# Seven pairs of input strips as seven block products each, and a triangular inversion in two blocks with its corner on TensorE

## The chip, the cores and the metric

The kernel runs on one core of a Trainium2 chip. The metric is the device time of one execution in microseconds (us), the median of several runs. Before the change it is 2264.03 us (three runs, 2262.74 to 2264.18). A second table of numbers comes from one profiled execution, whose times are counted from its first instruction.

## The reference

One decoder layer on 1024 tokens of width 1024, in float32: a SwiGLU half-step (ffn1), a mixer of three branches, and a second SwiGLU half-step (ffn2), each between two RMS norms. Cut to the mixer, which the change touches:

```python
u = rms_norm(h, mix_pre_g[l])
p_rwkv, p_swa, q_mem, gate_logits = _split(u @ w_in[l], IN_SIZES)
y_a = rwkv7_mix(p_rwkv, ...)            # recurrence over 1024 steps, 8 heads of 64
y_b = sliding_window_gqa_sinks(...)     # from p_swa, window 128
y_c = memory_cross_attention(...)       # from q_mem, 256 memory tokens
g_a, g_b, g_c = _split(jax.nn.sigmoid(gate_logits + gate_b[l]), (D, D, D))
merged = g_a * (y_a @ w_branch[l, 0]) + g_b * (y_b @ w_branch[l, 1]) + g_c * (y_c @ w_branch[l, 2])
h = h + rms_norm(merged @ w_out[l], mix_post_g[l])
```

## The kernel before, in words

**Products.** Activations lie feature-major: 8 blocks of 128 features (k) by 1024 tokens, in two halves of 512 (h = 0, 1). A float32 operand is split into a high part (a rounded copy, made by ScalarE, ACT: `w_hi`, line 288, or `split`, line 472) and a low part (the difference, made by VectorE, DVE: line 290 or 473). `mm3` (lines 364 to 366) makes a product of three matmuls: high by high, high by low, low by high. A *strip* is 128 output columns of a weight; `project` runs one strip over 8 k-blocks and both halves, 48 matmuls of 128x512. Weights come through five `w_raw` buffers of 256 KB (`raw`), and up to eight split operands are kept ahead of TensorE (PE) (`prefetch`); the order of the weights is `plan`'s list. DMAs of weights and results are nearly all issued by one in-order queue, SyncE's (SP).

**The feed-forward layers** already use a form of block product: two strips, two halves of K and two halves of the tokens are a 2x2 by 2x2 block product, made of seven products of 12 matmuls instead of eight, with sums of the weights (lines 315 to 321 for kind "pair") and sums of the input (`factors_part`, `factors_end`) made beside them, and sums of the results on the way out (`ffn_in_pair`).

**The mixer.** The `w_in` product has 48 strips: 14 for the recurrence (0 to 13), 10 for the two attentions (14 to 23, `att_block`), 24 for the gates (`gate_block`, a tanh on the way out). Half of strips 18, 19, 14 and 15, and four strips of the recurrence, are made earlier, while the first norm of the mixer runs. In order of the program then come:

- `rwkv_prep`: the other strips of the recurrence, their scans and norms, the triangular 64x64 matrices per chunk and head (16 chunks x 8 heads = 128 of them, products `ab`, line 1094, stored to `ab_d`), and the second halves of strips 18 and 19; `pk_d` and `bonus_d` are stored for later;
- `rwkv_invert`: all 128 matrices at once, one on each partition, loaded as rows of 64x64; 62 steps of two DVE operations (lines 1129 and 1130), each step adding an outer product of the j rows above by the 63 - j columns behind; a memset of the diagonal; one store to `inv_d`;
- strips 14 to 17 and 20 to 23, then gates 0 to 7;
- `rwkv_chain`: 16 chunks in sequence, small float32 matmuls on PE and short operations on the other engines, each chunk with its `f` and `dinv` loads; gates 8 and 9 are woven in;
- `rwkv_finish` and `attention` (8 memory blocks, 8 window blocks), between whose steps `fill(n, ...)` lets n matmuls of the remaining gates (10 to 23) and of two branches' projections pass. How many per block is written out by hand (`LUMPS` and the list in `mixer`); what is left follows the last block. `sums_beside` makes sums for ffn2's weights there.

**Order.** A scheduler orders each engine's instructions by priority (program order, moved ahead inside `high_priority(offset=...)`: 300 is `lead`, 1000 is `urgent`) as their inputs become ready; `keep_in_program_order` and `issue_after` fix single orders. Then each engine runs its list strictly. Tiles come from pools laid out from the left and the right end of each partition; a tile of a new pool waits for the last use of the tiles whose space it takes. PSUM has four banks for px, py, pgate, pq and the like, and four for the rest (pz, gram, z, y, ab).

**Norms.** `post_norm` ends in `acc` tiles, which are stored to `h1` (line 879) for the next residual; `pre_norm` (line 498) scales them into a tile `un` and splits it into u's high and low parts.

## Time and profile before

| | |
|---|---|
| three runs, median | 2264.03 us |
| profiled execution, its own span | 2260.2 us |
| TensorE busy | 2236.6 us, 99% |
| VectorE busy | 1652.0 us, 73% |
| ScalarE busy | 1000.2 us, 44% |
| DMA moved | 417.66 MB, 185 GB/s |
| granted TensorE clock, mean | 0.998 |

The profiled execution gives no time beside its span; the median of the runs is 3.8 us longer than that span. Stages by the profile: ffn1 up to about 650 us, then `rwkv_prep` to 885, inversion 908 to 1029 on VectorE beside strips and gates on PE, `rwkv_chain` 1048 to 1155, attention 1200 to 1448, ffn2's products from 1670.

How to read it: a row of a timeline has the start, the duration, the engine and line, operation and tiles, and in brackets the idle time before it and what ended it. A row of groups has the count, the busy time and the mean duration of one in ns. A row of waits has the total in us, the times, and the longest one. PE is the matmul side of TensorE and PEld its weight loads.

### The profile page before, as it was taken

How to read it: one execution, taken by the hardware profiler on the slowest of the kernel's cores; microseconds unless marked ns; L12 is line 12 of the kernel's file. 1: busy time of each engine (PE TensorE's matmuls, PEld its weight loads, DVE VectorE, ACT ScalarE, POOL GpSimd, SP SyncE). 2: the span in 40 equal slices, each digit the busy share in tenths (PEclk: the TensorE clock that was granted, in tenths of full speed). 3: DMA queues.
4: the chain of work that ended last, by engine and by line, in shares of the span. 5: the costliest groups of instructions: out<-in, count | busy, mean ns of one | idle time of the engine just before them, and what ended most of it. 6: DMA issues, size and time to landing. Idle time of an engine off the chain costs nothing.

```text
span 2260.2 us, 33447 instructions
## 1 busy us (share of the span) xinstructions
PE 2236.6 (99%) x11876; PEld 1840.4 (81%) x11876; DVE 1652.0 (73%) x2719; ACT 1000.2 (44%) x1880; POOL 58.1 (3%) x114
## 2 busy tenths in 40 slices
PE   8999999999999999999999999999999999999998
PEld 6888888888888788888888887788888888888887
DVE  6987777666698886995666576684898885656576
ACT  6533333454556653223454445334663233345451
POOL 0000000000000000001320000000000000000000
PEclk9999999999999999999999999999999999999999
DMA  8465666686654467325438885654565542347663
GB/s 291 157 210 168 215 212 208 214 276 207 191 173 149 117 143 183 118 93 194 144 113 289 266 278 186 209 177 136 173 214 188 189 168 90 116 165 250 204 196 122
DMA packets 280775, 417.66 MB, mean 185 GB/s; under 512 B 82304, under 2 KB 104320, under 8 KB 280352
## 3 DMA queue, kind: packets, MB, share of 16 engines
q1 hardware_dynamic: 272832, 400.26, 55.3%
q10 hardware_dynamic: 7776, 15.28, 2.0%
q8 instruction: 93, 1.52, 0.3%
q14 instruction: 74, 0.61, 0.1%
HBM read 284.89 MB, written 129.50 MB: 183 GB/s over the span
## 4 chain that ended last, share of the span: by engine, by line
PE 93%; DVE 4%; DMA 1%; ACT 1%; issue 1%; SPq 0%; DVEq 0%; ACTq 0%
PE px L365 7%; PE px L364 7%; PE px L366 7%; PE po L365 6%; PE po L366 6%; PE po L364 6%; PE pgate L364 4%; PE pgate L366 4%; PE pgate L365 4%; PE pz L365 3%; PE pz L364 3%; PE pz L366 3%; PE pb L364 2%; PE pb L365 2%; PE pb L366 2%; PE pr L364 2%
## 5 line engine op out<-in xcount | busy, mean ns | idle before, releaser
L288 ACT CAST w_hi<-w_raw 128x512 fp32r<-128x512 f32 x594 | 367.5, 620 | 734.5 <-PE px L365 159.7
L290 DVE TENSOR_TENSOR w_lo<-w_raw,w_hi 128x512 fp32r<-128x512 f32 x594 | 407.6, 687 | 196.0 <-ACT w_hi L288 175.2
L366 PE MATMUL po<-u,w_lo 128*128 128x512 f32 (+1 forms) x476 | 180.9, 380 | 0.0
L364 PE MATMUL po<-u,w_hi 128*128 128x512 f32 (+1 forms) x476 | 180.9, 380 | 0.0
L365 PE MATMUL po<-u,w_hi 128*128 128x512 f32 (+1 forms) x476 | 180.9, 380 | 0.0
L364 PE MATMUL pgate<-u,w_hi 128*128 128x512 f32 x384 | 153.2, 399 | 0.0
L366 PE MATMUL pgate<-u,w_lo 128*128 128x512 f32 x384 | 151.4, 394 | 0.0
L365 PE MATMUL pgate<-u,w_hi 128*128 128x512 f32 x384 | 149.8, 390 | 0.0
L365 PE MATMUL px<-f,w_hi 128*128 128x512 f32 x352 | 137.2, 390 | 1.0 <-DVE f L473 1.0
L364 PE MATMUL px<-u,w_hi 128*128 128x512 f32 x352 | 137.0, 389 | 0.8 <-DVE km L1442 0.8
L364 PE MATMUL px<-f,w_hi 128*128 128x512 f32 x352 | 137.1, 389 | 0.1
L366 PE MATMUL px<-u,w_lo 128*128 128x512 f32 x352 | 137.0, 389 | 0.0
L366 PE MATMUL px<-f,w_lo 128*128 128x512 f32 x352 | 137.0, 389 | 0.0
L365 PE MATMUL pz<-u,w_hi 128*128 128x512 f32 x352 | 137.0, 389 | 0.0
L365 PE MATMUL px<-u,w_hi 128*128 128x512 f32 x352 | 136.9, 389 | 0.0
L364 PE MATMUL pz<-u,w_hi 128*128 128x512 f32 x352 | 136.9, 389 | 0.0
L366 PE MATMUL pz<-u,w_lo 128*128 128x512 f32 x352 | 136.9, 389 | 0.0
L473 DVE TENSOR_TENSOR u<-hid,u 128x512 fp32r<-128x512 f32 x114 | 78.3, 690 | 46.5 <-ACT u L472 43.5
L364 PEld LDWEIGHTS po<-u,w_hi 128*128 128x128 f32 x476 | 89.5, 188 | 17.1
L365 PEld LDWEIGHTS po<-u,w_hi 128*128 128x128 f32 x476 | 89.5, 188 | 17.1
L366 PEld LDWEIGHTS po<-u,w_lo 128*128 128x128 f32 x476 | 89.5, 188 | 16.8
L472 ACT CAST u<-hid 128x512 fp32r<-128x512 f32 x114 | 70.7, 620 | 64.3 <-DMA hid<-form_d 55.7
(401 smaller groups left out, 5097.4 us busy)
## 6 DMA issues: line engine op xcount, KB each, us to landing
w_raw<-in_ffn_in SPq DMA_DIRECT2D x220, 256.0 KB
hid<-form_d SPq DMA_DIRECT2D x154, 256.0 KB
w_raw<-in_win SPq DMA_DIRECT2D x112, 256.0 KB
form_d<-g SPq DMA_DIRECT2D x88, 256.0 KB
w_raw<-ffn_sum_d SPq DMA_DIRECT2D x88, 256.0 KB
form_d<-h SPq DMA_DIRECT2D x66, 256.0 KB
w_raw<-in_ffn_out SPq DMA_DIRECT2D x66, 256.0 KB
gate_d<-gate SPq DMA_DIRECT2D x24, 512.0 KB
```

Of the source, the lines that this page charges most:

```text
L288: self.nc.scalar.copy(hi, x)
L290: self.split_last = self.nc.vector.tensor_tensor(lo, x, hi.bitcast(F32), ALU.subtract)
L364: mm(out, wh, xh, start=first, stop=False, **kw)
L365: mm(out, wh, xl, start=False, stop=False, **kw)
L366: self.last_mm = mm(out, wl, xh, start=False, stop=last, **kw)
L472: self.nc.scalar.copy(hi, x)
L473: self.nc.vector.tensor_tensor(lo, x, hi.bitcast(F32), ALU.subtract)
```

## The change

`pre_norm` scales the `acc` tile in place instead of into `un`, and stores it to `xn_d`. In the mixer, `mix_x` loads that input again in quarters (features low and high, tokens h = 0 and 1), four tiles for each of four k, through a pool `mix_parts` of five tiles; `mix_forms` makes four sums of them and splits each into high and low parts (32 tiles), with the lead of 300. Seven pairs of strips (16 and 17, 20 and 21, 22 and 23, and gates 2 to 9 in twos) are made by `win_pair` as seven block products; their weights get the four sums of kind "pair". Strips 14 and 15 and gates 0 and 1 stay as they are and now come first, behind `mix_forms`; then the inversion in program order, then the pairs.

The inversion runs on the two diagonal blocks of 32x32 of each matrix (30 steps of two operations, both blocks in one), stores the result, and a transposed copy of the first block to `turn_d`. Ahead of the pair with index 5, `rwkv_corner` loads the corner of the matrices and the two inverted blocks with rows on partitions (12 DMAs), multiplies them in two products of 128 small matmuls each (four groups of 32 partitions in turn), and stores the corner (4 DMAs).

Ten gates instead of eight are made ahead of the chain, the fill starts at gate 12 instead of 10, and the lumps are 42, 32, then 29 six times and 52 eight times, instead of 42, 34, 30 and 54.

```diff
-GATES_EARLY = 10
-LUMPS = (30, 54)
-GATES_FIRST = 8
+GATES_PLAIN = 2
+CORNER = 5
+GATES_FIRST = 10
+GATES_EARLY = 12
+LUMPS = (29, 52)
+WIN_PAIRS = ((16, 17), (20, 21), (22, 23)) + tuple((24 + g, 25 + g) for g in range(GATES_PLAIN, GATES_FIRST, 2))
...
-            t = pool.tile([P, TH], F32, tag="un", name="un", bufs=2)[:, : hi - lo]
-            self.nc.vector.scalar_tensor_tensor(t, xs[k], self.vec(gname, k), rs, ALU.mult, ALU.mult)
-            self.split(t, *(y[:, lo:hi] for y in u[k][h]))
+            self.nc.vector.scalar_tensor_tensor(xs[k], xs[k], self.vec(gname, k), rs, ALU.mult, ALU.mult)
+            self.split(xs[k], *(y[:, lo:hi] for y in u[k][h]))
+            self.nc.sync.dma_start(self.xn_d[:, k, h * TH + lo : h * TH + hi], xs[k])
...
+        blocks = x.rearrange("p (b r) -> p b r", b=2)[:, :, : H * C].rearrange("p b (s t) -> p b s t", t=C)[:, :, :, :H]
+        for j in range(1, H - 1):
+            n = H - 1 - j
+            tmp = pool.tile([P, H * H], F32, tag="itmp", name="itmp", bufs=1)
+            t = tmp[:, : 2 * j * n].rearrange("p (b a n) -> p b a n", b=2, n=n)
+            V.tensor_tensor(t, blocks[:, :, j : j + 1, j + 1 :].broadcast_to([P, 2, j, n]), blocks[:, :, 0:j, j : j + 1].broadcast_to([P, 2, j, n]), ALU.mult)
+            V.tensor_tensor(blocks[:, :, 0:j, j + 1 :], blocks[:, :, 0:j, j + 1 :], t, ALU.add)
...
+        up, turned, low, half, corner = (pool.tile([P, H, H], F32, name="i" + n, bufs=1) for n in ("up", "turned", "low", "half", "corner"))
+        for t, d in ((up, flat(ab_d)[:, :H, H:]), (turned, turn_d), (low, flat(inv_d)[:, H:, H:])):
+            for g in groups:
+                nc.sync.dma_start(t[g], d[g].rearrange("i s t -> s i t"))
+        for w, x, out in ((up, turned, half), (half, low, corner)):
+            for a in (0, H // 2):
+                ps = self.psum("corner").rearrange("p (i t) -> p i t", t=H)
+                for i in range(H // 2):
+                    for g in groups:
+                        self.tc.keep_in_program_order(nc.tensor.matmul(ps[g, i], w[g, a + i], x[g, a + i], start=True, stop=True))
+                nc.scalar.copy(out[:, a : a + H // 2], ps)
...
+            for k in range(KH):
+                x12, x22, x11, x21 = self.mix_x(k, parts) if k else first
+                V.tensor_tensor(x22, x22, x12, ALU.subtract)
+                V.tensor_tensor(x12, x12, x11, ALU.subtract)
+                V.tensor_tensor(x11, x22, x11, ALU.add)
+                V.tensor_tensor(x21, x21, x11, ALU.subtract)
+                for n, x in (("t2", x11), ("t1", x12), ("t3", x22), ("t4", x21)):
+                    self.split(x, *fs[n][k])
...
+        part(0, "b11", px, True)
+        x = kept(px)
+        part(1, "b21", py, True, True)
+        made(0, first, 0, py, x)
+        part(2, "t2", px)
+        u1 = kept(px)
+        part(3, "t1", pz, True)
+        z = kept(pz)
+        part(4, "t3", px)
+        made(1, second, 1, px, z)
+        part(5, "b22", pz, False, True)
+        made(0, first, 1, pz, u1)
+        part(6, "t4", px, False, True)
+        made(1, second, 0, px)
...
+            fs = self.mix_forms(u, forms, parts, first)
+            for f in FILL[ATT_FIRST:]:
+                self.att_block(f, u, att_d, out)
+            for g in range(GATES_PLAIN):
+                self.gate_block(g, u, gp, gate_d)
             with tc.tile_pool(reuse_waits="tile", name="inv", bufs=1) as pool:
-                self.rwkv_invert(pool, ab_d, inv_d)
-            for f in ATT_BLOCKS[ATT_FIRST:]:
-                self.att_block(f, u, att_d, lambda: gp.tile([P, T], F32, tag="gate", name="att", bufs=2))
-            for g in range(GATES_FIRST):
-                self.gate_block(g, u, gp, gate_d)
+                self.rwkv_invert(pool, ab_d, inv_d, turn_d)
+            for i in range(len(WIN_PAIRS)):
+                if i == CORNER:
+                    with tc.tile_pool(reuse_waits="tile", name="corner", bufs=1) as pool:
+                        self.rwkv_corner(pool, ab_d, inv_d, turn_d)
+                self.win_pair(i, fs, parts, out, att_d, gate_d)
+            over.close()
```

More of the change, by code (lines that the diff above doesn't have):

```diff
@@ L312, in operands @@
                 b1, b2 = self.raw(RAWS - 3), self.raw(RAWS - 4)
[L313 removed]
+                s = self.sum_tile()
                 with self.behind_up(kind):
@@ L1301, in rwkv_finish, with mix_x, mix_forms @@
                 self.fill(10, end)
+    def mix_x(self, k, parts):
+        out = [parts() for _ in range(4)]
+        for t, j, h in zip(out, (k, k + KH, k, k + KH), (1, 1, 0, 0)):
+            self.nc.sync.dma_start(t, self.xn_d[:, j, h * TH : (h + 1) * TH])
+        return out
+    def mix_forms(self, u, pool, parts, first):
+        V = self.nc.vector
+        tile = lambda: pool.tile([P, TH], F32R, tag="mix_form", name="mix_form", bufs=8 * KH)
+        fs = {"b11": [u[k][0] for k in range(KH)]}
+        for n, h in (("b21", 0), ("b22", 1)):
+            fs[n] = [u[k][h] for k in range(KH, KD)]
+        for n in ("t2", "t1", "t3", "t4"):
+            fs[n] = [(tile(), tile()) for _ in range(KH)]
+        with self.tc.high_priority(offset=self.lead):
+            for k in range(KH):
[6 more added lines that the diff above has]
+                    self.split(x, *fs[n][k])
+        return fs
@@ new lines, in win_pair, with part, kept, made @@
+    def win_pair(self, i, fs, parts, out, att_d, gate_d):
+        nc, V = self.nc, self.nc.vector
+        px, py, pz = self.psum("px"), self.psum("py"), self.psum("pz")
+        first, second = out(), out()
+        halves = (slice(0, TH), slice(TH, T))
+        strips = WIN_PAIRS[i]
+        def part(n, form, ps, *flags):
+            self.product(ps, self.take("win_pair", i), fs[form], *flags)
+        def kept(ps):
+            t = parts()
+            with self.tc.high_priority(offset=self.lead):
+                nc.scalar.copy(t, ps)
+            return t
+        def made(n, t, h, ps, x=None):
+            t, f = t[:, halves[h]], strips[n]
+            with self.tc.high_priority(offset=self.lead):
+                if x is not None:
+                    V.tensor_tensor(t, ps, x, ALU.add)
+                if f >= 24:
+                    g = f - 24
+                    nc.scalar.activation(t, ps if x is None else t, ACT.Tanh, scale=0.5, bias=self.half_gb[:, g : g + 1])
+                elif x is None:
+                    nc.scalar.copy(t, ps)
+        part(0, "b11", px, True)
[12 more added lines that the diff above has]
+        made(1, second, 0, px)
+        for f, t in zip(strips, (first, second)):
+            nc.sync.dma_start(gate_d[f - 24] if f >= 24 else att_d[ATT_ROW[f]], t)
@@ L1592, in mixer @@
         self.sg = cp.tile([P, T], F32, name="sg")
+        over = contextlib.ExitStack()
+        beside = over.enter_context(tc.tile_pool(reuse_waits="tile", name="mix_parts", bufs=5, side="right"))
+        parts = lambda: beside.tile([P, TH], F32, tag="part", name="part")
+        self.sum_tile = lambda: parts().rearrange("p (k c) -> p k c", c=P)
+        first = self.mix_x(0, parts)
         with tc.tile_pool(reuse_waits="tile", name="prep", bufs=8) as pool:
```

44 lines of the change are left out of this document (28 added, 16 removed).

## The prediction

> **What bounds the kernel now.** I read the profile's page first.
>
> ```profile
> span 2260.2 us, 33447 instructions
> PE 2236.6 (99%) x11876; PEld 1840.4 (81%) x11876; DVE 1652.0 (73%) x2719; ACT 1000.2 (44%) x1880; POOL 58.1 (3%) x114
> PE 93%; DVE 4%; DMA 1%; ACT 1%; issue 1%; SPq 0%; DVEq 0%; ACTq 0%
> ```
>
> The third line is the chain that ended last: 93% of it is TensorE (PE). Second view: busy time by stage, for the end of the prep, the inversion, the chain over chunks, and ffn2's in-pairs (columns: stretch, its length, then busy time and count of PE, PEld, DVE, ACT, POOL, the granted clock, the DMA share, GB/s).
>
> ```profile
> 885.00:923.00 38.00, 38.00 (x169) 31.48 (x168) 18.73 (x34) 8.90 (x17) 1.83 (x4) 1.00 0.68 209
> 923.00:1048.00 125.00, 125.00 (x556) 103.25 (x556) 106.17 (x124) 27.98 (x48) 1.58 (x4) 1.00 0.37 130
> 1048.00:1150.00 102.00, 101.53 (x1855) 84.77 (x1855) 63.09 (x158) 43.98 (x106) 34.71 (x59) 1.00 0.43 132
> 1670.00:2044.00 374.00, 374.00 (x1651) 309.53 (x1650) 274.67 (x438) 140.33 (x242) 0.00 (x0) 1.00 0.48 157
> ```
>
> PE has no gap in the stage that changes, although VectorE (DVE) is busy for 106 of 125 us there. The last row gives the price of one 128x512 matmul: 374.00/1651 = 0.2265 us. Third view: what PE waited for.
>
> ```profile
> PE pq L1355 <- DMA mkv<-in_mkv_k: 6.5, 1, 6.5
> PE msc L94 <- DVE gin L655: 1.6, 1, 1.6
> ...
> PE px L365 <- DVE f L473: 1.0, 1, 1.0
> ```
>
> So a change is worth what it takes from PE's own work, less what PE newly waits for.
>
> **The change, part by part.** *Products.* A pair of strips is 2 x 8 x 2 x 3 = 96 matmuls now (strips, k-blocks, token halves, the three hi/lo products); seven block products of 4 x 3 are 84. Seven pairs save 84 matmuls: 84 x 0.2265 = **-19.0 us**, all on the bound engine. The ffn2 row is the same form of pair (seven products, px, py and pz, four weight sums, eight operands ahead), and PE has no gap in it.
>
> *Corner on TensorE.* 2 products x 2 halves x 16 x 4 groups = 256 float32 matmuls of 32x32x32. The trace has none of that size; the nearest are these, of 64x64x64 (two row groups in turn, into one bank) and 128x64 by 64:
>
> ```profile
> 870.81 0.39 PE L364 MATMUL pq<-u,w_hi 128*128 128x512 f32 x1
> 871.44 2.08 PE L1094 MATMUL ab<-at,bk 64*64 64x64 f32 x64 [0.24 <-DVE bk L1080]
> 1057.02 0.69 PE z L1145 x16
> 1048.52 1.09 PE gram L1145 x16
> ```
>
> The second row: 2.08/64 = 32 ns; then 0.69/16 = 43 ns; 1.09/16 = 68 ns (a 64x128 one). The matmul of the change has half the columns and half the rows of the first, so from below half of that, 16 ns (256 x 16 = 4.1 us), and from above 43 ns (11.0 us). I take the nearest row unhalved, with 32 ns: **+8.2 us**, since with so little to stream the step from one instruction to the next may be all there is. The Trainium skill, "TensorE: Matmul & The Clock Gate", section "Wait — 56ns, not 53.3ns?", has a floor of about 25 ns from start to start for small matmuls (an estimate by it: 6.4 us) and, with hardware decode off, about 62 ns (15.9 us, which would eat most of the gain); the 32 ns row speaks against the second. "TensorEngine Tiling (Array Packing)", section "Gotcha 1: PSUM Pressure", says that different row tiles cannot access one PSUM bank at once; the corner's four groups do share a bank, which by that rule forbids the halved price; no row here shows it for 32-row tiles.
>
> *Inversion.* Now 124 dependent DVE operations; their durations, smallest and largest:
>
> ```profile
> L1129 DVE TENSOR_TENSOR itmp<-inv x62: 224/942/1191, 908.4 to 1028.6; 128x62 f32<-128x62 f32 x2, 128x122 f32<-128x122 f32 x2, 128x180 f32<-128x180 f32 x2, 128x236 f32<-128x236 f32 x2
> 908.36 0.22 DVE L1129 TENSOR_TENSOR itmp<-inv 128x62 f32<-128x62 f32 x1 [0.67 <-DMA inv<-ab_d]
> 967.27 1.19 DVE L1130 TENSOR_TENSOR inv<-inv,itmp 128x992 f32<-128x992 f32 x1
> ```
>
> That is 0.16 us + 1.04 ns per element. Two blocks of 32 at once need 60 operations over 2 x 9920 elements: 9.6 + 20.6 = 30 us, against 19.8 + 86.7 = 106 us. These 76 us of DVE lie beside PE, so they are worth nothing themselves; they pay for the sums:
>
> ```profile
> L290 DVE TENSOR_TENSOR w_lo<-w_raw,w_hi 128x512 fp32r<-128x512 f32 x594 | 407.6, 687 | 196.0 <-ACT w_hi L288 175.2 <-PE po L365 8.0 <-PE y L1145 4.9
> L288 ACT CAST w_hi<-w_raw 128x512 fp32r<-128x512 f32 x594 | 367.5, 620 | 734.5 <-PE px L365 159.7 <-PE pz L365 111.6 <-DVE w_raw L317 98.7
> ```
>
> The input's forms: 16 sums and 16 splits, 32 x 0.687 = 22 us of DVE, 16 x 0.62 = 10 us of ACT. A pair has 14 DVE operations where two strips have 4: 9.6 us within its 84 x 0.2265 = 19.0 us of PE; on ACT 7 casts, 3 copies and 4 outputs, about 9 us. DVE from 885 us to the chain then has 18.7 + 106.2 - 106 + 30 + 22 + 7 x 6.9 = 119 us in about 171: not the bound, if the order is right.
>
> *Are the forms in time?* Between strip 15 and the first product on a made form (t2) stand two gates and two products on b11 and b21, 96 + 24 matmuls = 27.2 us. Strip 15 is done at 895.9, so t2 is wanted at 923.1. The forms' 64 KB a partition come to lie, as I read the pools, where the prep's planes were, whose last stores leave late:
>
> ```profile
> 895.92 0.58 ACT L1496 COPY att<-pq 128x512 f32<-128x512 f32 x1
> 894.48 0.42 SPq L1105 DMA_DIRECT2D bonus_d<-m  x1
> 897.15 1.42 SPq L1497 DMA_DIRECT2D att_d<-att  x3
> 450.62 4.17 DMA hid<-form_d
> SPq L279 <- DVE w_lo L290: 176.8, 64, 7.1
> ```
>
> From about 899 to 923 are 24 us for 22 us of forms, and the inputs come four tiles a round through five buffers, a load taking some 4.2 us. t3 and t4 are wanted only 5.4 and 10.9 us later, and sums may run before the space is free. Bounds: nothing, and four rounds end to end, 17 us (worked out below). I take **+1.0 us**, the length of the like wait in ffn_in (the row of px waiting for f), because DVE has room and the forms go ahead by a lead of 300. What is queued behind a late form on DVE is the weights' low parts; eight operands ahead cover 8 x 12 x 0.2265 = 21.7 us of PE.
>
> *Is the corner's input in time?* The corner is due at 895.9 + 21.7 + 5 x 19.0 = 1012.6 us. The inversion, sharing DVE half and half with the pairs, takes some 60 us from the forms' end: 983 or so. Then 2 MB go out, and 12 loads of 1024 pieces of 128 bytes come in:
>
> ```profile
> 1029.25 0.33 SPq L1132 DMA_DIRECT2D inv_d<-inv  x1
> 1036.21 1.32 SPq L1153 DMA_DIRECT2D dinv<-inv_d  x2
> DMA packets 5083, 2.06 MB, mean 206 GB/s; under 512 B 4653, under 2 KB 4653, under 8 KB 5082
> q1 hardware_dynamic: 5082, 2.04, 84.7%
> ```
>
> The store takes 7 us. The last two rows are a 10 us stretch (874 to 884): 5,082 mostly small packets in 84.7% of it, so 12,288 in some 20 us. 983 + 7 + 20 = 1010: just in time. 0 is taken; the bound is 10 us, with pair 5's products queued behind the corner on PE.
>
> *Rest.* The normalised input is scaled in place and stored, 16 DMAs of 256 KB more. In place, the scaling must wait for the residual's store of the same tile:
>
> ```profile
> 697.77 0.32 SPq L879 DMA_DIRECT2D h<-acc  x1
> 709.30 1.41 DVE L498 SCALAR_TENSOR_TENSOR un<-acc,vecs,rs 128x512 f32<-128x512 f32 x2
> ```
>
> 11.5 us lie between, against 4.2 us for a load of that size: hidden; uncovered it would be one wait of about 4 us, with the u tiles and the first strips behind it. Two gates move ahead of the chain: by the counts in the code the fill holds 960 matmuls instead of 1056, and 880 instead of 904 are asked for, so 80 instead of 152 are left after the last block. In a block the fill hides the softmax, and at the end the load of y:
>
> ```profile
> 1360.89 1.66 DVE L150 TENSOR_SCALAR sc<-sc,st 128x128 f32<-128x128 f32 x8
> 1371.57 1.09 PE L97 MATMUL ptr<-ident,sc 128*128 128x128 f32 x8
> 1446.45 1.93 PE pv L94 x16
> 1458.24 0.68 DVE L473 TENSOR_TENSOR y<-yin,y 128x512 fp32r<-128x512 f32 x1
> ```
>
> Nine us between the scaled scores and their transposes, of which two matmuls fewer take 0.5; y's first half is split 10.5 us after the last block, 80 matmuls last 18.1. Zero for both. The chain's first tiles lie partly where the forms were: 0, or one load of about 4 us.
>
> **Sum:** -19.0 + 8.2 + 1.0 = -9.8 us, against the profiled span 2260.2: 2250.4. The median of the runs shown, 2264.0, is 3.8 us above that span (what lies around it, which stays): **2254.2 us**.
>
> **Rivals.** *Cheaper still:* the four groups of the corner overlap (16 ns), nothing waits, and the 1.6 us that msc waits for gin go: -19.0 + 4.1 - 1.6 = -16.5, 2247.5. For: the ab row has two groups in turn. Against: 32 ns may be the step between instructions.
>
> *The gain is eaten:* the corner's operands come 6 us late or the chain's first tiles 4 us late, or the corner costs 11.0: -9.8 + 3 to 6, 2257 to 2262, about 2260. For: the estimate of 1010 against 1012.6. Against: PE's order is made by readiness; in the trace a matmul of strip 18 (pq, 870.81) stands ahead of the ab products that wait for DVE, and so pair 5's products, which come behind the corner, could be put ahead of it.
>
> *Slower:* the forms are late. Each round waits for its loads (4.2 us), these behind weight loads that hold SP's queue (176.8/64 = 2.8 us on average), then 8 x 0.687 = 5.5 us: 12.5 us a round. From 899: 5.5 + 3 x 12.5, so 942 us, against 923 to 925: PE idles 17 us. -19.0 + 8.2 + 17 = +6, 2270. It decides once the wait is over 15.3 us (10.8 of gain, and 4.5 for 0.2%). For: five buffers, one in-order queue. Against: tiles come free one by one, most of them before 899, so the first rounds may be over by then.
>
> That PE stops being the bound is excluded by DVE's 9.6 and ACT's 9 us in a pair's 19.0.
>
> **Chances.** Forecast (2249.5 to 2258) 0.62; cheaper still 0.10; the gain eaten 0.18; forms late, slower 0.10. About 0.2% (4.5 us) is what a measurement can tell from no change, so faster means under 2259.5: 0.62 + 0.10 = 0.72; the eaten case, centred on that bound, counts as same, 0.18, since as much of the forecast's tail lies above the bound as of this case under it; slower 0.10. Range: from the cheaper case, 2247, to 2266, between the eaten case and the slower one.
>
> **What would show it.** PE's busy time down by about 11 us; from the end of strip 15 to the chain's first gram about 2.7 + 8.2 + 1 = 12 us more than now, and 96 x 0.2265 = 21.7 us less between there and the end of the fill. 256 small matmuls in 8 us in one stretch, with no wait on low or turned ahead; no PE wait on mix_form over 2 us; DVE's inversion ended by 990. Wrong: a PE gap of over 5 us at the first pair, at the corner or at the chain's start, or a corner of over 12 us.

## The result, and the profile after

The change makes the kernel slower: 2275.52 us (four runs, 2272.09 to 2279.02) against 2263.39 us of the kernel before beside it, ratio 1.0054, 95% interval 1.0039 to 1.0068. The profiled execution spans 2272.3 us, 12.1 us more than before; the sum of the prediction was 9.8 us less. So 21.9 us are to be found.

The page after: the span, busy time by engine, and the chain that ended last.

```profile
span 2272.3 us, 34532 instructions
PE 2233.4 (98%) x12304; PEld 1834.1 (81%) x12304; DVE 1638.7 (72%) x2757; ACT 1031.7 (45%) x1934; POOL 58.5 (3%) x114
PE 89%; DVE 6%; DMA 2%; issue 2%; ACT 1%; SPq 0%; ACTq 0%; DVEq 0%
```

TensorE's work did fall (2236.6 to 2233.4 us), but its share of the chain that ended last fell from 93 to 89%: PE now waits. The waits of PE (total, times, longest):

```profile
PE z L1176 <- DVE sv L1270: 7.8, 7, 1.3
...
PE pz L372 <- ACT w_hi L296: 4.0, 1, 4.0
...
PE pz L374 <- issue: 1.4, 1, 1.4
...
PE corner L1161 <- issue: 0.9, 2, 0.5
```

PE's timeline at the corner (like instructions in a row are merged, x147 is 147 of them):

```profile
1033.69 1.44 PE L1161 MATMUL corner<-iturned,iup 32*32 32x32 f32 x147
1035.50 1.07 PE L1161 MATMUL corner<-iturned,iup 32*32 32x32 f32 x103 [0.37 <-issue]
...
1041.53 1.29 PE L1161 MATMUL corner<-ilow,ihalf 32*32 32x32 f32 x129
1043.33 1.24 PE L1161 MATMUL corner<-ilow,ihalf 32*32 32x32 f32 x123 [0.52 <-issue]
```

Of the waits, in the first row the chain over chunks waits (`z` is a small product of a chunk, `sv` the state that VectorE hands to it). In the second the first product on a made form waits; what came last there is the high part of its weight, whose ScalarE cast stood among the casts of the last forms. The third row follows the corner, the fourth is the corner itself. Busy time by stage, columns as in the prediction (the eighth number is the granted clock):

```profile
923.00:926.00 3.00, 0.61 (x3) 0.19 (x1) 2.98 (x6) 0.70 (x2) 0.00 (x0) 1.00 0.50 190
926.00:933.00 7.00, 5.29 (x12) 3.70 (x13) 7.00 (x13) 5.28 (x11) 0.00 (x0) 0.53 0.19 63
...
1130.00:1178.00 48.00, 40.59 (x851) 34.45 (x847) 29.98 (x76) 21.16 (x51) 17.11 (x29) 1.00 0.42 130
```

After the forms' wait the clock is 0.53 for 7 us: 12 matmuls pass where 31 would. And the chain, which had hardly any idle time before, has 7.4 us of it in its last 48 us. The chain begins 29.3 us later (its first product, `gram`, at 1077.7 against 1048.4), where the two gates made ahead of it, less the pairs' saving, are 21.7 - 19.0 = 2.7 us; it lasts the same 107 us, although by the trace's count 69 matmuls of gates lie in it instead of 108. The other 39 were worked off just ahead of it.

### The profile page after: what moved, and what is told of

Read it like the earlier page. It is cut to its first block, busy times and chain, and to the rows that moved or that the text cites. A ratio compares the mean times of both kernels' runs of the same rounds, so it can differ in the third digit from the quotient of the medians.

```text
span 2272.3 us, 34532 instructions
## 1 busy us (share of the span) xinstructions
PE 2233.4 (98%) x12304; PEld 1834.1 (81%) x12304; DVE 1638.7 (72%) x2757; ACT 1031.7 (45%) x1934; POOL 58.5 (3%) x114
## 4 chain that ended last, share of the span: by engine, by line
PE 89%; DVE 6%; DMA 2%; issue 2%; ACT 1%; SPq 0%; ACTq 0%; DVEq 0%
PE px L372 8%; PE px L373 8%; PE px L374 8%; PE po L373 6%; PE po L374 6%; PE po L372 6%; PE pz L374 4%; PE pz L372 4%; PE pz L373 4%; PE pgate L372 2%; PE pgate L374 2%; PE pgate L373 2%; PE pr L372 2%; PE pr L373 2%; PE pr L374 2%; PE pb L372 2%
## 5 line engine op out<-in xcount | busy, mean ns | idle before, releaser
L296 ACT CAST w_hi<-w_raw 128x512 fp32r<-128x512 f32 x608 | 375.8, 620 | 711.9 <-PE px L373 182.1
L298 DVE TENSOR_TENSOR w_lo<-w_raw,w_hi 128x512 fp32r<-128x512 f32 x608 | 417.8, 689 | 203.6 <-ACT w_hi L296 185.7
L372 PE MATMUL px<-u,w_hi 128*128 128x512 f32 x380 | 148.2, 390 | 0.8 <-DVE km L1544 0.8
L372 PE MATMUL pz<-u,w_hi 128*128 128x512 f32 x380 | 148.1, 390 | 0.0
L373 PE MATMUL px<-u,w_hi 128*128 128x512 f32 x380 | 148.0, 389 | 0.0
L374 PE MATMUL px<-u,w_lo 128*128 128x512 f32 x380 | 148.0, 389 | 0.0
L373 PE MATMUL pz<-u,w_hi 128*128 128x512 f32 x380 | 147.9, 389 | 0.0
L374 PE MATMUL pz<-u,w_lo 128*128 128x512 f32 x380 | 147.8, 389 | 0.0
L372 PE MATMUL pgate<-u,w_hi 128*128 128x512 f32 x256 | 103.9, 406 | 0.0
L374 PEld LDWEIGHTS po<-u,w_lo 128*128 128x128 f32 x476 | 89.5, 188 | 16.8
L374 PE MATMUL pgate<-u,w_lo 128*128 128x512 f32 x256 | 100.4, 392 | 0.0
L373 PE MATMUL pgate<-u,w_hi 128*128 128x512 f32 x256 | 99.8, 390 | 0.0
```

Of the source, the lines that this page charges most:

```text
L296: self.nc.scalar.copy(hi, x)
L298: self.split_last = self.nc.vector.tensor_tensor(lo, x, hi.bitcast(F32), ALU.subtract)
L372: mm(out, wh, xh, start=first, stop=False, **kw)
L373: mm(out, wh, xl, start=False, stop=False, **kw)
L374: self.last_mm = mm(out, wl, xh, start=False, stop=last, **kw)
```

## The experiments

Each was timed in five rounds beside the kernel before (medians 2262.9 to 2264.6 us), and ratios are to that one. "The kernel after" is 2275.5, 1.0054 [1.0039, 1.0068]. The intervals of e5, e6, e2 and e14 overlap that one, and e3's touches it, so their gains of 3 to 5 us are not clear of noise one by one; those of e9, e4, e7, e11 and e15 to e18 are. My theory: three losses, the forms' wait with its clock (7 us), the chain's fill (8 us), the corner (6 to 9 us). Rivals: the corner is the whole loss; the inversion's operations hold up the forms; the losses only move.

**e1_inv_late.** The inversion's first operation waits for the forms' last split (`split` now returns its low part's instruction):

```diff
-                    self.split(x, *fs[n][k])
+                    self.formed = self.split(x, *fs[n][k])
...
+            with self.tc.issue_after(self.formed.ins) if j == 1 else contextlib.nullcontext():
```

> The first operation of the two-block inversion is put behind the last split of the forms on VectorE; nothing else is edited, nothing is left out. Theory A (the forms are late because the inversion's operations of 0.45 to 0.65 us stand between the forms' sums and splits on VectorE, which is busy all of 925 to 940): the one wait of 4.0 us of TensorE on the high part of a weight ahead of pz goes to under 1 us, the granted clock stays at 1.00 between 925 and 935, and the time falls by 6 to 8 us, to 2267 to 2270 (ratio to the kernel before 1.002 to 1.003). Theory B (the forms are late because their input comes late through five buffers and SyncE's queue): the wait stays at 3 us or more, the clock still falls to 0.50 after it, and the time stays at 2274 to 2277 (1.005). Under both, the inversion ends some 15 us later, at 995 or so, and the corner begins at the same place.

2275.98 us, 1.0053 [1.0041, 1.0065]: no gain. Waits of PE in that run:

```profile
PE corner L1162 <- issue: 4.0, 2, 2.2
PE pz L374 <- DVE w_lo L298: 2.3, 1, 2.3
PE pz L372 <- ACT w_hi L296: 1.4, 1, 1.4
```

The forms' wait is in two pieces and nearly as long (3.7 us), although the inversion's first operation now starts at 932.5 instead of 906.2, and the corner now waits 4.0 us. VectorE's order is not the cause; theory A of this run falls.

**e5_mixq.** The other half of the question, the loads' queue:

```diff
-            self.nc.sync.dma_start(t, self.xn_d[:, j, h * TH : (h + 1) * TH])
+            (self.nc.gpsimd if k else self.nc.sync).dma_start(t, self.xn_d[:, j, h * TH : (h + 1) * TH])
```

> The loads of the forms' second to fourth rounds go out on GpSimd's queue instead of SyncE's; nothing is left out. In the kernel after, the rounds' sums began at 907.2, 914.6 and 922.1, and their loads stood on SyncE behind three stores of strip 15, the 2 MB load of the inversion and two stores of gates. Theory A (that place in the queue makes the forms late): the rounds come 3 to 7 us earlier, the first product on t1 or t2 begins at 924 or before, the wait of 4.0 us and the granted clock of 0.50 behind it go, and the time falls by 5 to 7 us, to 2268.5 to 2270.5 (ratio to the kernel before 1.0022 to 1.0031). Theory B (the rounds are paced by VectorE and by the buffers of one round being freed by the splits of the round before): the period of 7.5 us stays, the wait is 3 us or more, and the time stays at 2274 to 2277.

2272.31 us, 1.0042 [1.0030, 1.0054]: 3.2 us less by the medians, about half of what was expected. The first group below is of the kernel after, where three rounds of sums begin at 907.2 and, by the trace, 914.6 and 922.1; the second fence is a wait of this run.

```profile
L1352 DVE TENSOR_TENSOR part<-part x3: 683/685/693, 907.2 to 922.1; 128x512 f32<-128x512 f32 x3
```

```profile
PE px L372 <- ACT part L1374: 4.9, 1, 4.9
```

The rounds keep their period here (906.6 to 921.3), since a load waits for a buffer that the round before frees, and now it is the copy of px into one of the same five buffers that PE waits for. So what is short seems to be neither the queue nor the engine but the five `part` buffers, which forms, weight sums and results share.

**e9_early_x.** So the inputs of rounds 3 and 4 go where the last forms will be written (a `slot` is a tile of tag `mix_form`; the forms' tiles are then taken k by k). The edit of e5 is in it as well: all loads but those of the first round go out on GpSimd's queue.

```diff
+            slot = lambda: tile(F32)
+            xs = [first, self.mix_x(1, parts), self.mix_x(2, slot)]
+            x3 = [slot() for _ in range(3)]
+            order = iter((x3[1], x3[2], x3[0], parts()))
+            xs.append(self.mix_x(3, lambda: next(order)))
...
-                x12, x22, x11, x21 = self.mix_x(k, parts) if k else first
...
+                x12, x22, x11, x21 = xs[k]
```

> The forms' inputs of rounds 2 to 4 no longer wait for the buffers of the round before: round 2 goes into the buffers that round 1 leaves, seven of the eight tiles of rounds 3 and 4 go into slots of forms that are written last, all loads on GpSimd's queue at once. Nothing is left out. The run with that queue alone kept the period of about 7 us a round, and the wait moved to px, whose copy wanted one of the same five buffers. Theory A (the buffers' turn-around makes the forms late): the 24 operations of rounds 2 to 4 follow each other on VectorE from about 905, the last split is done by 923, TensorE waits under 1 us, the granted clock stays at 1.00, and the time falls by 5 to 7 us against the kernel after, to 2268.5 to 2270.5 (ratio 1.0022 to 1.0031). Theory B (VectorE itself, with the inversion and the weights' low parts between, is too slow, or the copies of px still want a buffer that a form holds): 3 us or more of waiting stay, 2273 to 2276.

2268.14 us, 1.0025 [1.0015, 1.0034]: 7.4 us less than the kernel after by the medians, 6.6 by the ratios. The same windows in this run:

```profile
923.00:926.00 3.00, 3.00 (x15) 2.28 (x14) 3.00 (x6) 3.00 (x7) 0.00 (x0) 1.00 0.39 115
926.00:933.00 7.00, 7.00 (x32) 5.81 (x31) 7.00 (x15) 3.63 (x7) 0.00 (x0) 1.00 0.41 145
```

No idle time, 32 matmuls instead of 12, the clock at 1.00: wait and slow clock go together. The first sum for the weights, which takes one of the five buffers too, now begins at 915.4 instead of 922.7. That the buffers' turn-around was the cause, and not the queue, is shown best by e7 and e11 below, which differ in the buffers alone. The trace that was kept is of the slowest of the nine executions (2275.1 us): its chain begins at 1073.2 instead of 1077.7, and it loses those 4.5 us again behind the chain, so the 7.4 us stand in the medians and not in this trace.

**e6_plain4.** The other way to give the forms time:

```diff
-GATES_PLAIN = 2
-CORNER = 5
+GATES_PLAIN = 4
+CORNER = 4
```

> Two gates more are made as plain strips ahead of the pairs, and six pairs are left instead of seven; the corner stands ahead of the last but one pair as before. Nothing is left out. 12 matmuls more are 2.7 us; the forms are wanted 21.7 us later than now. If the forms' lateness costs the 4.2 us of waiting and the 2.9 us of halved clock that the trace after shows, the wait goes and the time falls by 4.4 us, to 2271 (ratio 1.0034). If the halved clock has another cause than the wait, it stays somewhere between 920 and 950, and the time falls by 1.5 us only, to 2274. If the lateness is moved on with the pairs (VectorE being overloaded by sums, splits and inversion together), a wait of 3 us stands before the first product on t1 or t2 again, at about 945, and the time rises by 2 to 3 us.

2271.74 us, 1.0043 [1.0028, 1.0057]. The forms' wait is gone from the trace and the median is near the expected one; but the corner waits 5.0 us there (0.9 in the kernel after), and the ratio says 2.5 us less rather than 4.4.

**e2_chain_in.** Now the chain. SyncE's queue in the kernel after, at the chain's start:

```profile
1068.85 0.33 SPq L1403 DMA_DIRECT2D gate_d<-att  x1
1069.27 0.38 SPq L1182 DMA_DIRECT2D f<-pk_d  x1
1074.35 0.32 SPq L1403 DMA_DIRECT2D gate_d<-att  x1
1074.76 1.28 SPq L1184 DMA_DIRECT2D dinv<-inv_d  x2
```

Chunk 0's loads go out behind the last pair's stores. Until they are there, PE does not stand still: it works off 39 of the 96 matmuls of gates 10 and 11, which were meant as cover for the chain.

```diff
+                if i == len(WIN_PAIRS) - 1:
+                    pin = ins.enter_context(tc.tile_pool(reuse_waits="tile", name="chain_in", bufs=2))
+                    self.pin = pin
+                    n0 = self.chain_in(pin, pk_d, inv_d, 0)
                 self.win_pair(i, fs, parts, out, att_d, gate_d)
```

> The chain's first inputs (f and dinv) get a pool of their own, in the space that the corner's tiles leave, and chunk 0's loads stand ahead of the last pair in program order; nothing is left out. Theory A (the chain ran out of fill because 17 of the matmuls of gates 10 and 11 were spent on the wait for chunk 0's loads, which stood behind the last pair's stores on SyncE): the first gram starts at 1073 to 1074 instead of 1077.7, the 17 matmuls lie in the chain, its idle time falls by 17 x 0.2265 = 3.9 us, and the time falls by 3 to 5 us, to about 2271.5 (ratio 1.0035). Theory B (the chain's late chunks wait for VectorE's work, however much fill there is): the chain starts earlier by 4 us but the same idle stands in it, and as the fill is only moved, the time stays within 1 us of 2275.5 less the 0 to 1 us of waiting at its start.

2272.14 us, 1.0034 [1.0023, 1.0045]: 3.4 us less; the first gram stands at 1073.3, 86 matmuls lie in the chain instead of 69, and the waits for sv fall from 7.8 to 4.1 us. So 17 of the 39 matmuls were spent on the loads' place in the queue; 22 are still worked off ahead of the chain.

**e3_gate13.** The same by more fill:

```diff
-GATES_EARLY = 12
-LUMPS = (29, 52)
+GATES_EARLY = 13
+LUMPS = (28, 50)
```

> One gate more (12) is given to the chain as fill, the fill behind it starts at gate 13, and the lumps are 28 and 50 instead of 29 and 52; nothing is left out. Theory A (the idle time of some 8 us in the chain's last chunks is want of fill): 48 matmuls more cover it, TensorE's busy time between 1130 and 1180 goes from about 0.83 to 0.98, and the time falls by 6 to 9 us, to 2267 to 2270 (1.002 to 1.003). Theory B (the waits only move on: the blocks of the attention, with one or two matmuls less each and 54 instead of 80 left behind them, then wait as long): the chain is busy, but the attention and the branches behind it lose 4 to 8 us, and the time stays at 2272 to 2277.

2270.37 us, 1.0029 [1.0019, 1.0039]: 5.2 us less. The window of the chain and a wait in the attention:

```profile
1130.00:1178.00 48.00, 47.96 (x900) 40.43 (x895) 29.69 (x75) 21.53 (x52) 17.47 (x29) 1.00 0.45 139
```

```profile
PE msc L98 <- DVE gin L663: 3.5, 1, 3.5
```

The chain is full (47.96 of 48, where it was 40.59). A part comes back as a longer wait of the scores (`msc`, 1.4 us in the kernel after): theory A holds, and a share of B.

**e4_no_corner.** `pass` in place of `self.rwkv_corner(...)`.

> The corner is left out altogether: its 12 loads, 256 small matmuls, 4 copies and 4 stores; the chain then reads matrices whose corner is not inverted, at the same cost. It prices the corner. By the prediction's sum, 8.2 us go: 2267.3. By the stretches of the trace after (1.44, 1.07, 1.29 and 1.24 us, and 1.4 us in which TensorE waited for what the profile does not name), 6.4 us go: 2269. If the corner also holds up SyncE's queue, and by that the chain's start, the 17 matmuls of the gates stay in the chain as well, and 10 to 12 us go: 2264 to 2266. If the time falls by over 13 us, the corner alone is the cause of the loss and the forms' wait is not.

2267.15 us, 1.0006 [0.9998, 1.0015]: 8.4 us less by the medians, 10.9 by the ratios; ten more matmuls of gates are kept for the chain (79 instead of 69), so a part of this is the chain's. That the corner is the whole loss falls: without it the kernel is still not faster than before, though it has 84 matmuls less.

**e8_corner_only.** The kernel before with the new `rwkv_invert` and `rwkv_corner`, and, with `CORNER = 5`:

```diff
             for g in range(GATES_FIRST):
+                if g == CORNER:
+                    with tc.tile_pool(reuse_waits="tile", name="corner", bufs=1) as pool:
+                        self.rwkv_corner(pool, ab_d, inv_d, turn_d)
                 self.gate_block(g, u, gp, gate_d)
```

> The kernel before, with the two-block inversion and the corner alone: no pairs, no forms, no stores of the normalised input; the corner stands ahead of gate 5, its matmuls in one stretch. Nothing is left out. It prices inversion and corner beside undisturbed strips. By the prediction's 8.2 us: 2271.7 (ratio 1.0036). By the stretches of the trace after, 512 small instructions at about 10 ns, 5.0 us, and 1 to 2 us at their edges: 2269.5 to 2270.5 (1.0027 to 1.0031). If the corner also holds back the chain's loads on SyncE here: 2274 or more (1.0047).

2277.72 us, 1.0064 [1.0051, 1.0077]: 14.4 us, more than the whole change loses. PE's timeline, then the queues of the stretch 1016 to 1029 (packets, MB, share), then a window:

```profile
1015.98 1.86 PE L1155 MATMUL corner<-iturned,iup 32*32 32x32 f32 x194
1019.78 0.73 PE L1155 MATMUL corner<-iturned,iup 32*32 32x32 f32 x62 [1.93 <-issue]
1020.36 0.96 PE L1155 MATMUL corner<-ilow,ihalf 32*32 32x32 f32 x66
1023.34 1.93 PE L1155 MATMUL corner<-ilow,ihalf 32*32 32x32 f32 x128 [2.02 <-issue]
1026.80 1.07 PE L1155 MATMUL corner<-ilow,ihalf 32*32 32x32 f32 x62 [1.52 <-issue]
```

```profile
q8 instruction: 4, 0.07, 1.9%
```

```profile
1020.00:1031.00 11.00, 7.46 (x323) 6.49 (x310) 0.00 (x0) 1.75 (x3) 0.00 (x0) 0.53 0.19 42
```

PE stops three times, for 1.5 to 2.0 us, after the first 194 matmul instructions and then after every 128, for nothing that the profile names, while four transfers of instructions land (0.07 MB, some 16 KB each). From 1020 to 1031 the clock is 0.53. The Trainium skill, "Runtime: NRT & Kernel Launch", section "Instruction fetch mechanics", says that an engine's instructions come in blocks of 16 KiB, or 256, and that this is mostly hidden; the size agrees (128 matmuls and as many weight loads), the hiding does not, if the stops are these transfers.

**e10_corner_woven** and **e13_corner_halves** (on the kernel before, as e8) test that. In the first, two groups of four small matmuls follow each three matmuls of gates 5 and 6; in the second, 64 small matmuls follow each twelve (the `yield` then stands ahead of each 64). `mm3` advances the generator.

```diff
+                    yield
+                    with self.tc.issue_after(self.last_mm.ins):
                         for g in groups:
                             self.tc.keep_in_program_order(nc.tensor.matmul(ps[g, i], w[g, a + i], x[g, a + i], start=True, stop=True))
```

> As the run with the corner alone, but two groups of four small matmuls follow each three matmuls of gates 5 and 6, instead of 256 in one stretch. Nothing is left out; the counts are the same. In the run with the corner alone TensorE stopped three times, for 1.9, 2.0 and 1.5 us, after some 128 small instructions each, and in each of these stretches of 2 to 3.6 us one transfer of instructions (16 KB) landed; the granted clock fell to 0.50 after the first stop. Theory A (TensorE eats small instructions faster than their transfers bring them): woven, the stops and the low clock go, the corner costs its 5 to 6 us, and the time falls from 2277.7 to 2269 to 2270 (ratio 1.0025 to 1.0030). Theory B (the stops are the corner's own dependence on its copies and loads, or small matmuls lower the clock by themselves): the stops stay or are longer, as the products are still in order, and the time stays above 2275.

2287.35 us, 1.0109 [1.0096, 1.0122]: a miss of both theories. No stops, the clock at 1.00, and 10 us more:

```profile
1017.79 0.33 PE L1162 MATMUL corner<-iturned,iup 32*32 32x32 f32 x16
1018.04 0.50 PE L366 MATMUL pgate<-u,w_hi 128*128 128x512 f32 x1
1018.38 0.40 PE L367 MATMUL pgate<-u,w_hi 128*128 128x512 f32 x1
1018.62 0.39 PE L368 MATMUL pgate<-u,w_lo 128*128 128x512 f32 x1
1018.94 0.33 PE L1162 MATMUL corner<-iturned,iup 32*32 32x32 f32 x16
```

A period is 1.15 us, where three matmuls of 0.2265 and sixteen instructions of 10 ns make 0.84: there and back costs 0.31 us, 32 times 10 us. The Trainium skill, "TensorEngine Tiling (Array Packing)", section "Key Properties", says that a change of the tiling mode drains TensorE; the trace shows a price that fits with this, not the drain itself. The chain, which begins at 1074.8 here, waits 8.3 us for sv. With 5 us for the corner's own instructions that makes 23 of the 24.1 us by which this run is longer than the kernel before.

> The kernel before with two-block inversion and corner alone, as e8, but the corner's 256 small matmuls go in four stretches of 64 with 12 matmuls of gates between. Nothing is left out. Theory A (the stops are for instructions, 16 KB each, and a stretch of 64 matmuls fits what is there): no stop, the granted clock stays at 1.00, the corner costs 512 x 9 ns + 4 x 0.33 us = 6 us, against 11.8 us and a slow clock in one stretch: 2269 to 2270.5 (ratio 1.0026 to 1.0032). Theory B (the stops are for the copies or the loads): they stay, 2275 to 2278 (1.005 to 1.0065).

2269.70 us, 1.0029 [1.0017, 1.0041], as theory A said:

```profile
1019.09 1.29 PE L1166 MATMUL corner<-iturned,iup 32*32 32x32 f32 x128
1023.25 0.57 PE L1166 MATMUL corner<-iturned,iup 32*32 32x32 f32 x42
1024.06 0.93 PE L1166 MATMUL corner<-iturned,iup 32*32 32x32 f32 x86 [0.23 <-issue]
1027.88 1.29 PE L1166 MATMUL corner<-ilow,ihalf 32*32 32x32 f32 x128
1032.04 1.29 PE L1166 MATMUL corner<-ilow,ihalf 32*32 32x32 f32 x128
```

Four stretches of 1.3 us, stops of 0.2 us in all: the same arithmetic for 6.8 us instead of 14.4. So one long stretch makes the stops, and large matmuls between short ones take them away. That they are for instructions is likely but not shown: it rests on this and on the transfers' times, and no run changed the transfers themselves.

**e7_three** (e5, e2 and e3 together) gave 2268.37 us, 1.0024 [1.0015, 1.0032]. I expected 2260.5 to 2262.5 if the loads' queue was what made the forms late, and 2267.5 to 2269.5 if it was not. The forms are still late:

```profile
PE px L372 <- ACT part L1378: 5.0, 1, 5.0
```

**e11_four** (e9, e2 and e3 together, so e7 with e9's buffers) and **e12_four_woven** (with the corner woven by eights).

> The early inputs of the forms, chunk 0's loads ahead of the last pair, and one gate more for the chain with lumps of 28 and 50, all at once. Nothing is left out. If the losses are the forms' wait with its clock (6 to 7 us), the chain's fill (8 us), and the corner, which stays: 2275.5 - 6.5 - 8 + 2 to 3 us for new waits in the attention, as the run with one gate more showed (3.5 us for the memory block's scores): 2262.5 to 2264 (ratio 0.9996 to 1.0003). If the forms' wait stays: 2268 to 2270 as with the three edits before (1.002 to 1.003).

2263.68 us, 0.9998 [0.9989, 1.0006]: the three mendings give 11.8 us, which only brings back the time of the kernel before. Against e7 it is 4.7 us less, with no wait at the forms, and the two intervals are apart: that is the price of the buffers alone. The corner stays, and the attention waits for its scores (msc 2.5, sc 1.5 us, the clock 0.98 over 180 us).

> As the last, and the corner's loads stand ahead of the pair with index 4, its matmuls two groups at a time behind each three matmuls from that pair's fifth product on. Nothing is left out. If the stops for instructions (0.9 and 1.4 us in the kernel after) and the edges of the corner go, and its input is there at about 1012: another 2 to 4 us, 2259 to 2262 (ratio 0.998 to 0.9993), under the kernel before. If its input is not there by then, TensorE waits for it, as each product now stands behind the group ahead of it: 2265 to 2272.

2278.51 us, 1.0069 [1.0057, 1.0081], outside both branches. The weaving costs here too, and the corner's input is late:

```profile
PE corner L1169 <- DMA iturned<-turn_d: 6.6, 4, 4.6
```

No run separates the two.

**e14_six_const.** Gates 8 and 9 go back to the chain:

```diff
-CORNER = 5
-GATES_FIRST = 10
-GATES_EARLY = 12
-LUMPS = (29, 52)
+CORNER = 4
+GATES_FIRST = 8
+GATES_EARLY = 11
+LUMPS = (30, 54)
```

> The kernel after with other constants alone: gates 8 and 9 are left to the chain, so six pairs instead of seven, the fill behind the chain from gate 11, the lumps of the kernel before (30 and 54, first 42 and 34), and the corner ahead of the last but one pair. Nothing is left out. 12 matmuls more cost 2.7 us. If the loss beyond the forms and the corner is want of fill in the chain and the attention (8 and 4 us), the time falls by 8 to 10 us, to 2266 to 2268 (ratio 1.0012 to 1.002). If that loss is something else, it rises by 2.7 us, to 2278. The corner comes in one stretch here, which may take back 3 to 5 us.

2271.10 us, 1.0039 [1.0025, 1.0052]: 4.4 us less by the medians in spite of 2.7 us of matmuls more; the chain's waits are gone, and the corner, now in one stretch, has three stops as in e8, 6.5 us together.

**e15_six**: e14's constants with e9, e2 and the corner as in e13, from the fifth product of pair 4 on.

> As e14, with the forms' early inputs of e9, chunk 0's loads ahead of the corner's pair's successor as in e2, and the corner in four stretches of 64 between the products of the fifth and sixth pair. Nothing is left out. Six pairs save 72 x 0.2265 = 16.3 us, the corner costs 6, 1.2 us goes for the first wait of pair 0 and 1 to 2 us for the rest: 2263.4 - 16.3 + 6 + 3 = 2256 (ratio 0.9967). If the attention's waits and low clock of the run with four edits stay in spite of the fill: 2260 to 2263 (0.9985 to 0.9998).

2264.72 us, 1.0008 [1.0000, 1.0017], 8.7 us over the sum. Waits and a window:

```profile
PE corner L1168 <- DMA iturned<-turn_d: 6.4, 4, 2.9
...
PE corner L1168 <- DMA ilow<-inv_d: 1.3, 1, 1.3
```

```profile
1000.00:1020.00 20.00, 13.60 (x167) 10.82 (x166) 2.73 (x5) 4.14 (x7) 0.00 (x0) 0.74 0.56 93
```

The corner's loads stand between those of the weights on SyncE, from 986 to 1022.

**e16_six_loads** and **e17_six_later** (the first stretch two products later):

```diff
-                nc.sync.dma_start(t[g], d[g].rearrange("i s t -> s i t"))
+                with self.tc.high_priority(offset=self.urgent):
+                    nc.sync.dma_start(t[g], d[g].rearrange("i s t -> s i t"))
```

> As e15, and the twelve loads of the corner go out with a priority that puts them ahead of the weights' loads on SyncE. Nothing is left out. If the corner's input was late on that queue, TensorE's 7.7 us of waiting and the 4 to 5 us of low clock behind it go, and the time falls from 2264.7 by 8 to 11 us, to 2254 to 2257 (ratio 0.996 to 0.9975). If the twelve loads of 1024 pieces are late by themselves (some 20 us by the estimate of the prediction, from 980), they land at 1000 at the best and the first products wait 0 to 2 us. If the weights behind them come late, a wait on w_hi of 2 to 5 us stands near 1000 and half of the gain is lost.

2253.62 us, 0.9952 [0.9939, 0.9966]: faster than both kernels.

> As e16, with the corner's first stretch behind the last product of the fifth pair, 5 us later. Nothing is left out. If e16 has no waits at the corner, this differs by less than 1.5 us from it, the chain being due only at 1050; if the input is late still, it is faster by 2 to 5 us. Either way 2254 to 2258 (0.996 to 0.998).

2254.36 us, 0.9955 [0.9942, 0.9967]: no difference. Windows of e16's forms, corner and chain:

```profile
923.00:945.00 22.00, 22.00 (x99) 18.21 (x98) 21.68 (x43) 8.02 (x16) 0.00 (x0) 1.00 0.40 135
1006.00:1022.00 16.00, 15.82 (x558) 12.61 (x557) 5.55 (x9) 7.98 (x14) 0.00 (x0) 1.00 0.49 153
1100.00:1150.00 50.00, 49.68 (x925) 41.91 (x926) 31.63 (x78) 20.68 (x49) 18.12 (x31) 1.00 0.38 118
```

PE is full, or nearly so, at all three places, and the clock is 1.00.

**e18_seven**: e16 with the seven pairs, gates and lumps of the kernel after.

> As e16 with the changed kernel's own constants: seven pairs, gates 10 and 11 for the chain, lumps 29 and 52. Nothing is left out. 12 matmuls fewer are 2.7 us less. If the smaller fill costs nothing as long as chunk 0 starts without waiting (96 matmuls stay in the chain): 2251 (ratio 0.994). If the chain and the attention lack fill in any case, as their idle time of 8 and 4 us in the kernel after says: the chain has 96 against 112 matmuls, so 3 to 4 us, and the attention 1 to 3 us: 2254 to 2258 (0.9955 to 0.997).

2254.75 us, 0.9963 [0.9949, 0.9976]: 2.7 us less work and no gain over e16. The two intervals overlap; which is better is not settled. The chain has no waits for sv in this trace; what differs is the clock in the attention (0.97 from 1390 to 1480, where e16 has 1.00), so the smaller fill may cost there what the seventh pair saves. No run isolates it.

## Why the prediction was wrong

Forecast 2254.2 in 2247 to 2266, measured 2275.5: slower, outside the range.

The traces of before and after account for the whole difference of 12.1 us, stage by stage. The last product ahead of the changed stage (`rk`) starts 0.8 us later than before. From there to the first gram it takes 28.5 us more, of which 2.7 were planned and 8.8 are the 39 matmuls of fill; 17.0 us are lost, some 7 at the forms and some 10 at the corner. The chain takes as long as before (0.4 us less) with those 39 matmuls fewer in it: 8.4 us are lost. Behind the chain the span is 16.8 us shorter, where 96 matmuls fewer are 21.7: 4.9 us are lost. So -19.0 + 0.8 + 17.0 + 8.4 + 4.9 = 12.1. Now the steps of the prediction.

- **Products, -19.0: right, as far as shown.** In e16 six pairs save 72 x 0.2265 = 16.3 us; with the 6.8 us of e13 for the corner that is 9.5 us less, measured 10.9 less (0.9952). No run has the pairs without everything else.
- **"Are the forms in time?", +1.0: wrong, the first step that failed.** It cost 7.4 us by e9's median, 4.7 by e11 against e7. The step counted DVE's 22 us against 24 us of time, and did not follow the buffers, whose rounds go end to end. The rival "forms late" had the five buffers in it, but its rounds were too long (4.2 + 2.8 + 5.5 = 12.5 us, measured 7.5) and so was its wait (17, measured 4.0). What neither had is the clock behind the wait, about 3 us more: 12 matmuls in 7 us. The reason given, that "DVE has room and the forms go ahead by a lead of 300", did not bear on it: in e1 the inversion left DVE to the forms, and they were as late.
- **Corner, +8.2: near the cost in place, and by luck.** It cost 8.4 us by medians (e4), some 10 by the traces. But 2.08/64 was read as one matmul; the corner's 256 matmuls are 512 rows of the trace, so a float32 matmul is two, and the row meant 65 ns a matmul, or 16.6 us for 256. The corner's rows go at 10 ns (1.29 us for 128), 5 us together. The stops (0.9 and 1.4 us) and the changes between 32x32 and 128x128 make up most of the rest; no term of the sum stood for either. Of the two rules of the Trainium skill weighed there, the floor of 25 ns ("TensorE: Matmul & The Clock Gate", section "Wait — 56ns, not 53.3ns?") does not hold here for instructions of four groups in turn, which start 10 ns apart; and four groups that share a bank run at that rate, so the rule on banks ("TensorEngine Tiling (Array Packing)", section "Gotcha 1: PSUM Pressure") cost no time that the trace shows.
- **"Is the corner's input in time?", 0: right for PE, wrong in its working.** The estimate had the loads landed at 1010. In the kernel after, the last four of them went out on SP's queue only from 1023.5 to 1027, and the others stood between loads of weights. PE lost nothing by it, since the scheduler put pair 5's first products ahead of the corner (its first long stretch starts at 1033.7), which the prediction had as an argument against its rival. With the corner's start fixed the lateness cost 7.7 us of waiting (e15), and e16 shows that the place in the queue was the cause.
- **"The chain's first tiles ...: 0, or one load of about 4 us": the load was late, and the price was another.** PE was not idle for it but spent fill, 17 of the 39 matmuls by e2; the idle time stood some 50 us and more behind, as 7.8 us on sv. e2 and e3 took 3.4 and 5.2 us of that away, neither alone clear of noise, but e11 has no such wait left. The step "Two gates move ahead of the chain ... Zero for both" failed too: it looked at the attention and at what is left over, not at the chain's own cover.
- **Attention, 0: wrong by a few us.** It is the likely place of most of the 4.9 us behind the chain: the trace after has waits of 1.4 and 0.8 us and a clock of 0.98 from 1390 to 1480 there, and e3, e9 and e11 show waits of 1.5 to 3.5 us with a clock of 0.96 to 0.99. What these cost by themselves was not measured.
- **Inversion, 0: right.** It ended at 982 (due by 990).
- **In-place scaling and stores, 0: nothing speaks against it.** The last `rk` product starts at 883.7, as in e8, which has neither of the two, and 0.8 us later than before.

The range failed since its parts were taken as alternatives: forms late, or the chain's tiles, or the corner. They came together, and each was priced by its wait alone, without the clock and without the fill that it eats.

## What to carry to other kernels

Count a buffer's turn-around, not only an engine's work: a producer in rounds is as late as the load that waits for the round before to free its buffers. A late input on a bound engine with movable fill shows no idle time where it is late; look for the fill that went too early, and for the stage that misses it. And a saving in a stage without gaps is real, but it is paid out only when nothing new waits: here 10.9 us came after the forms' buffers, the chain's fill, the loads' place in the queue, and the length of a stretch of small matmuls were put right.

## What was not expected of the hardware

- 512 matmul instructions of 32x32 in one stretch, 10 ns apart, stopped three times for 1.5 to 2.0 us (e8); four stretches of 128 with twelve large matmuls between them had 0.2 us of stops (e13).
- A change from 128x512 to 32x32 matmuls and back costs 0.31 us (e10).
- One wait of 4 us was followed by a granted clock of 0.53 for 7 us: the matmuls behind it start 0.43 us apart instead of 0.23 (the kernel after). Among small matmuls a shorter stop was enough: in e8 the clock is 0.50 from 1021 on, behind one stop of 1.9 us. A stop of 1.4 us among large matmuls, and seven waits of at most 1.3 us in the chain, left it at 1.00 (the kernel after).
